# A two-layer hybrid decoder: GLA state products in halves, attention strips zeroed once, later holds for two mixer products

## Chip, core, metric

One core of one Trainium2 chip runs the whole program. The metric is the device time of one execution in microseconds; the median of the runs counts.

## What is computed

Two layers of a decoder on 512 tokens of width 2048, in float32. Each layer normalises its input, multiplies it with one wide matrix, feeds slices of the result to four mixers (Conformer convolution, RG-LRU, sparse attention, gated linear attention), gates and joins their outputs and multiplies them with a second matrix.

```python
h = rmsnorm(x, pre_g)
proj = h @ w_in                      # 2048 -> 5916, split among the mixers and their gates
o_a = gla_mixer(...); o_b = rglru_mixer(...); o_c = nsa_mixer(...); o_d = conformer_mixer(...)
mixed = group_rmsnorm(concat(o_a, o_b, o_c, o_d), branch_g) * silu(z)
x = x + rmsnorm(mixed @ w_out, post_g)
```

The change is in the GLA mixer, which works in 8 chunks of 64 tokens, with 4 heads of 64 key and 128 value channels:

```python
attn = where(causal, q_dec @ (k * exp(-bcum)).T, 0)        # within a chunk
dstate = (k * exp(b_last - bcum)).T @ v                    # what a chunk adds to the state
state = decay * state + dstate                             # chunk after chunk
o = attn @ v + q_dec @ state_before
```

## The kernel before

Every large product is made three times in a reduced float32 format: an operand is split into a high half (a copy on ScalarE, ACT) and a low half (a difference on VectorE, DVE, or GpSimd, POOL), and `mm3` (L227) adds high x high, high x low and low x high. In the profile H and L are the halves of the layer's input, whi and wlo those of the weights, shi and slo those of mixer data. GLA's own products run in full float32; one shows as two records of PE.

A layer goes like this: four columns of the Conformer's gate (tiles f), then columns of 128 outputs one after another (`proj`, L277, tile pfm), each of 16 blocks of the 2048 inputs, 3 products a block. Column numbers count these from 0: 0 to 3 Conformer values, 4 to 7 RG-LRU, 8 to 11 attention keys and values, 12 and 13 queries, 14 to 17 GLA queries and keys, 18 and 19 queries, 20 to 35 the gates z. A block of token-major columns (tm) and the GLA values (gv) stand in between. The output projection (out_ps) ends the layer; its first two columns are taken up to the 12th block before the last four blocks, which are GLA's.

The mixers are generators; `advance` (L267) lets the first in the list run a few steps between columns. Who stands where in an engine's queue is then decided by the scheduler of the tile framework from priorities and its own model of durations: weight loads and their splits have the band "first", the weight products the band "last", mixer work lies between. PE's weight products therefore fill what mixers leave.

`LAG` (L62) names four places where mixer products are held by hand: with `late` (L215) they are put down, and `release` (L220) makes them follow one given product of a column, (column, block). Held are the Conformer's variance sum, the first of its pointwise products (pw_ps), the first transposes of GLA (klt_ps0) and the first state product (ds_ps).

`gla` (L600) works on two pairs of heads, p = 0 and 1. For each: decays (ga, gb, gm, ge), decayed queries gqz and keys gkd, then transposed keys (klt_ps, copied to gklt), scores of two heads (at_ps, L668), each head's scores written through a causal mask into a strip gat that GpSimd has zeroed (L664, L665, L670), seven state products (ds_ps, L681) whose results DVE adds to the running state gsp (L686, L134), and outputs (go_ps) from gat and from gqz with gsp. State products contract 64 rows: even chunks lie on rows 0 to 63 of PE, odd ones on rows 64 to 127. The strips come from a ring of five buffers, tag "pt", which weights, sums and attention use too; "qg" is a ring of four that holds the halves of the second query pair.

After `gla` its output is normalised (`group_norm`, L296: square, sum on PE gn_ps, square root on ACT, reciprocal on DVE), gated on POOL, and split by `put_h` (L255) into the halves that the output projection reads.

Of the kernel before, what the change touches and what calls it, by code (L numbers as in the profile page):

```python
# [21 lines left out]
P = 128  # L22
# [26 lines left out]
CONF, LRU, NSA, GLA = range(4)  # L49
# [9 lines left out]
PS_A, PS_B = (0, 1, 2, 3, 4, 5), (0, 3)  # L59


LAG = {"var_ps": (13, 13), "pw_ps": (15, 1), "klt_ps0": (31, 15), "ds_ps": (32, 4)}  # L62


class Trunk:
# [148 lines left out]
    @contextmanager  # L214
    def late(self, name):  # L215
        self.lag = name if name in LAG else None
        yield
        self.lag = None

    def release(self, ins, col, k):  # L220
        for name, at in LAG.items():
            if at == (col, k):
                for i in self.held.pop(name, ()):
                    self.tc.add_manual_dep(i, ins.name, mybir.DependencyInfo(
                        mybir.DependencyClass.NoSync, mybir.DependencyReason.DATA), reason="late")
# [374 lines left out]
    def gla(self, qk, gv, fg):  # L600
        dve, act, gp = self.dve, self.act, self.gp
        wfg = self.strip("pt", "wfg", 512)
        self.nc.sync.dma_start(wfg[:96, :256], self.a["w_fg2"][self.l])
        wf3 = self.strip("pt", "wf3", 512, F32R)
        self.high_low_high(wf3[:96, :256], wfg[:96, :256], dve)
        fg3 = self.strip("pt", "fg3", 512, F32R)
        self.high_high_low(fg3[:, :384].rearrange("p (b r n) -> p b r n", b=4, r=3),
                           fg.rearrange("p (b n) -> p b n", b=4), 16, dve)
        spt = self.quad("x0", "gsp")
        qzt = self.quad("x1", "gqz")  # L610
        Y = self.Y[GLA] = self.quad("t3", "ygla")
        pf = self.bank("fg_ps")
        for b in range(4):
            self.tr(pf[:96, b * P:(b + 1) * P], fg3[:, b * 96:(b + 1) * 96].bitcast(F32), self.ident)
        fgT = self.strip("pt", "fgT", 512, F32R)
        act(fgT[:96], pf[:96, :], AF.Copy)
        pfg = []
        for p in range(2):
            ps = self.bank("fg2_ps")
            self.mm(ps, wf3[:96, p * P:(p + 1) * P], fgT[:96])  # L620
            pfg.append(ps)
        for p in range(2):
            q, k = [qk[:, (2 * p + i) * 512:(2 * p + i + 1) * 512] for i in range(2)]
            ps = pfg[p]
            bf = self.col(V_BFG + p)
            a_, m_, b_, e_ = [self.strip("yv", n) for n in ("ga", "gm", "gb", "ge")]
            act(a_, ps, AF.Abs, bias=bf)
            self.ts(dve, m_, ps, bf, 0.0, ALU.add, ALU.min)
            act(a_, a_, AF.Exp, scale=-1.0)
            act(a_, a_, AF.Ln, bias=self.one)  # L630
            gp.tensor_sub(m_, m_, a_)
            gp.memset(e_, 1.0)
            gp.memset(e_.rearrange("p (c t) -> p c t", c=8)[:, :, 0:1], 0.0)
            dve.tensor_tensor_scan(b_, e_, m_, 0.0, op0=ALU.mult, op1=ALU.add)
            yield 3.0
            b3 = b_.rearrange("p (c t) -> p c t", c=8)
            act(a_, b_, AF.Exp, scale=1.0 / 16)
            a3 = a_.rearrange("p (c t) -> p c t", c=8)
            dec = self.sm.tile([P, 8], F32, tag="dec", name="dec")
            dve.tensor_copy(dec, a3[:, :, 63])  # L640
            qz = qzt[:, 1024 * p:1024 * p + 1024]
            qd = qz.rearrange("p (c h t) -> p c h t", c=8, h=2)
            gp.memset(qz, 0.0)
            for h in range(2):
                r = slice(64 * h, 64 * h + 64)
                dve.tensor_mul(qd[r, :, h, :], q[r].rearrange("p (c t) -> p c t", c=8), a3[r])
            yield 2.0
            act(e_, b_, AF.Exp, scale=-1.0 / 16)
            kd = self.strip("pt", "gkd")
            gp.tensor_mul(kd, k, e_)  # L650
            dve.tensor_sub(m_.rearrange("p (c t) -> p c t", c=8), b3[:, :, 63:64].to_broadcast([P, 8, 64]), b3)
            act(m_, m_, AF.Exp, scale=1.0 / 16)
            gp.tensor_mul(k, k, m_)
            ps = self.bank("klt_ps")
            with self.late(f"klt_ps{p}"):
                for b in range(4):
                    self.tr(ps[:, b * P:(b + 1) * P], k[:, b * P:(b + 1) * P], self.ident)
            klT = self.strip("pt", "gklt")
            act(klT, ps, AF.Copy)
            yield 3.0  # L660
            at = []
            for h in range(2):
                r = slice(64 * h, 64 * h + 64)
                t = self.strip("pt", f"gat{h}")  # L664
                gp.memset(t, 0.0)  # L665
                ps = self.bank("at_ps")
                for b in range(4):
                    self.mm(ps[:, b * P:(b + 1) * P], kd[r, b * P:(b + 1) * P], qd[r, 2 * b:2 * b + 2, h, :],  # L668
                            b == 0, b == 3, skip_group_check=True)
                dve.copy_predicated(t.rearrange("p (b c) -> p b c", b=4),  # L670
                                    self.glam[:, None, :].to_broadcast([P, 4, P]),
                                    ps.rearrange("p (b c) -> p b c", b=4))
                at.append(t)
                yield 2.0
            sp = spt[:, 1024 * p:1024 * p + 1024].rearrange("p (c e) -> p c e", c=8)
            for c in range(7):
                ps = self.bank("ds_ps")
                r = slice(64 * (c % 2), 64 * (c % 2) + 64)
                b = c // 2
                with self.late(None if p + c else "ds_ps"):  # L680
                    self.mm(ps[:, :256], klT[r, b * P:(b + 1) * P], gv[r, 512 * b + 256 * p:512 * b + 256 * p + 256])  # L681
                for h in range(2):
                    r = slice(64 * h, 64 * h + 64)
                    d = ps[r, h * P:(h + 1) * P]
                    if c == 0:
                        dve.tensor_copy(sp[r, c + 1], d)  # L686
                    else:
                        self.stt(sp[r, c + 1], sp[r, c], dec[r, c:c + 1], d, ALU.mult, ALU.add)
                yield 1.5
            for i in range(2):  # L690
                po = self.bank("go_ps", self.op, "op")
                o4 = po.rearrange("p (h c t) -> p h c t", h=2, c=4)
                for h in range(2):
                    for b in range(2):
                        v0 = 512 * (2 * i + b) + (2 * p + h) * P
                        self.mm(po[:, h * 256 + b * P:h * 256 + (b + 1) * P], gv[:, v0:v0 + P],
                                at[h][:, (2 * i + b) * P:(2 * i + b + 1) * P], h + b == 0, False,
                                skip_group_check=True)
                for c in range(4):
                    if i + c > 0:  # L700
                        self.mm(o4[:, :, c, :], sp[:, 4 * i + c], qd[:, 4 * i + c], False, c == 3,
                                skip_group_check=True)
                for h in range(2):
                    c0 = (2 * p + h) * 512 + 256 * i
                    act(Y[:, c0:c0 + 256], po[:, h * 256:(h + 1) * 256], AF.Copy)
                yield 3.0
        yield from self.group_norm(GLA)
# [44 lines left out]
    def layer(self, l, xs):  # L752
        nc, a, dve, act, gp = self.nc, self.a, self.dve, self.act, self.gp
# [11 lines left out]
        first = [self.bank(f"f{i}", self.acc, "acc") for i in range(4)]  # L765
# [8 lines left out]
        for u, t in steps:  # L774
# [7 lines left out]
            for k in (2 * u, 2 * u + 1):  # L782
# [3 lines left out]
                with self.band("last"):  # L786
                    for i in range(4):
# [3 lines left out]
                                 skip_group_check=len(halves) > 1)  # L791
# [21 lines left out]
        for c in range(4):  # L813
            yv = self.strip("yv", "yv", 542)
            gp.memset(yv[:, :30], 0.0)
            ps = self.bank("pfm") if c < 2 else None
# [53 lines left out]
        for i, c in enumerate((NSA_KC, NSA_VC, NSA_KS, NSA_KW)):  # L870
            self.scaled(kv[i], self.proj(c))
            if i >= 2:
                hv, lv, zv = [t.rearrange("p (j r) -> p j r", j=4) for t in (KH, KL, kv[i])]
                r = slice((i - 2) * P, (i - 1) * P)
# [24 lines left out]
        for p in range(2):  # L899
            for i, (c, s) in enumerate(((GLA_Q, 0.125), (GLA_K, 1.0))):  # L900
                ps = self.proj(c + p * P)
# [3 lines left out]
        gv = self.quad("t6", "gv")  # L905
# [43 lines left out]
            self.load_vec(l + 1)  # L949
        M, N = [None] * KT, [None] * KT  # L950
        for i in range(KT):
            self.put_h(M, N, i, self.Y[i // 4][:, (i % 4) * 512:(i % 4 + 1) * 512], None)


        xs = [self.quad(tag, "xs") for tag in self.XTAGS]
# [153 lines left out]
```

## Time and profile before

| | |
|---|---|
| runs | 1632.26 to 1633.25 us, median 1632.89 |
| profiled execution | 1629.83 us |
| its span, first to last instruction | 1628.0 us |
| PE, DVE, ACT, POOL busy | 98%, 63%, 45%, 29% of the span |
| mean granted clock of PE | 0.994 |
| data moved | 165.54 MB, mean 102 GB/s |

Busy is not bound: PE's matmuls overlap, so that the distance of their starts is their price, and the ends that the profile shows are modelled. Idle time of the other engines costs nothing as long as PE does not wait for them.

### The profile page before, as it was taken

To read this page: it belongs to the slowest core of one execution; us is meant where nothing else is said; L and a number is where in the kernel's file an instruction comes from. 1 tells how busy PE (TensorE), PEld (TensorE's weight loads), DVE (VectorE), ACT (ScalarE), POOL (GpSimd) and SP (SyncE) were. 2 spreads that over 40 slices of the span, in tenths; PEclk is the share of its full clock that TensorE was granted. 3 is DMA by queue.
4 is the path that set the end of the run, shared out by engine and by line. 5 is a ranking of instruction groups with operands and counts; after the bars stand their busy time and mean duration, and the time that the engine had idled before them with its cause. 6 is when DMAs were issued, how large, how long until landed. Compare 5 with 4: busy or idle time off the path is not lost.

```text
span 1628.0 us, 22310 instructions
## 1 busy us (share of the span) xinstructions
PE 1591.1 (98%) x8380; PEld 1351.7 (83%) x8380; DVE 1024.5 (63%) x1654; ACT 727.1 (45%) x1313; POOL 471.9 (29%) x399
## 2 busy tenths in 40 slices
PE   8999999999999999999989999999999999999996
PEld 6889887998888777888888898879988887788886
DVE  8588986478564758111496889854976667571114
ACT  7322465454455635333453224654544555453331
POOL 1452242212123413222145522411121235132223
PEclk9999999999999999999999999999999999999998
DMA  7322322422112213442333222234221212134323
GB/s 251 104 92 83 117 78 99 158 75 88 53 66 69 90 53 128 157 136 98 111 130 110 99 90 91 91 117 143 78 74 57 78 59 77 63 117 155 121 99 117
DMA packets 54861, 165.54 MB, mean 102 GB/s; under 512 B 5920, under 2 KB 14816, under 8 KB 54752
## 3 DMA queue, kind: packets, MB, share of 16 engines
q1 hardware_dynamic: 53376, 162.79, 29.9%
q8 instruction: 66, 1.08, 0.3%
q10 hardware_dynamic: 1376, 1.31, 0.2%
q14 instruction: 43, 0.35, 0.1%
HBM read 155.69 MB, written 8.39 MB: 101 GB/s over the span
## 4 chain that ended last, share of the span: by engine, by line
PE 88%; DVE 7%; ACT 2%; DMA 2%; issue 1%; POOL 0%; SPq 0%; DVEq 0%; POOLq 0%; ACTq 0%
PE pfm L203 44%; PE out_ps L203 20%; PE gv L203 6%; PE tm L203 3%; PE f L203 2%; PE o_ps L203 2%; PE s_ps L203 2%; PE pw_ps L203 1%; DVE L L134 1%; PE go_ps L203 1%; PE pt_ps L209 1%; DVE wlo L148 1%; PE ch_ps L203 1%; PE ds_ps L203 1%; PE gn_ps L203 1%
## 5 line engine op out<-in xcount | busy, mean ns | idle before, releaser
L147 ACT ACTIVATE whi<-raw 128x512 fp32r<-128x512 f32 (+1 forms) x506 | 309.3, 616 | 615.5 <-PE pfm L203 305.6
L148 POOL TENSOR_TENSOR wlo<-raw,whi 128x512 fp32r<-128x512 f32 (+1 forms) x211 | 276.5, 1311 | 805.1 <-ACT whi L147 761.9
L203 PE MATMUL pfm<-H,whi 128*128 128x512 f32 x1152 | 452.7, 393 | 0.0
L203 PE MATMUL pfm<-H,wlo 128*128 128x512 f32 x1152 | 452.0, 392 | 0.3 <-POOL wlo L148 0.3
L203 PE MATMUL pfm<-L,whi 128*128 128x512 f32 x1152 | 452.0, 392 | 0.0
L148 DVE TENSOR_TENSOR wlo<-raw,whi 128x512 fp32r<-128x512 f32 (+1 forms) x295 | 225.8, 769 | 318.9 <-ACT whi L147 308.5
L203 PEld LDWEIGHTS pfm<-H,wlo 128*128 128x128 f32 x1152 | 216.7, 188 | 46.3 <-issue 1.0
L203 PEld LDWEIGHTS pfm<-H,whi 128*128 128x128 f32 x1152 | 216.6, 188 | 44.9 <-issue 0.7
L203 PEld LDWEIGHTS pfm<-L,whi 128*128 128x128 f32 x1152 | 216.6, 188 | 44.7 <-issue 0.4
L203 PE MATMUL out_ps<-L,whi 128*128 128x512 f32 (+1 forms) x552 | 200.9, 364 | 0.7 <-DVE L L262 0.7
L203 PE MATMUL out_ps<-H,wlo 128*128 128x512 f32 (+1 forms) x552 | 200.7, 365 | 0.0
L203 PE MATMUL out_ps<-H,whi 128*128 128x512 f32 (+1 forms) x552 | 200.3, 365 | 0.0
L134 DVE SCALAR_TENSOR_TENSOR cv_ps<-yv,vec,cv_ps 128x512 f32<-128x512 f32 x232 | 175.0, 754 | 6.8
L203 PEld LDWEIGHTS out_ps<-L,whi 128*128 128x128 f32 x552 | 104.0, 188 | 17.7 <-DVE L L262 1.1
L203 PEld LDWEIGHTS out_ps<-H,whi 128*128 128x128 f32 x552 | 104.0, 188 | 16.7
L203 PEld LDWEIGHTS out_ps<-H,wlo 128*128 128x128 f32 x552 | 104.0, 188 | 16.4
L234 DVE RECIPROCAL gn_ps<-gn_ps 128x512 f32<-128x512 f32 x32 | 107.4, 3356 | 9.6 <-ACT gn_ps L233 9.6
L203 PE MATMUL gv<-wlo,H 128*128 128x256 f32 x256 | 72.7, 284 | 0.0
L203 PE MATMUL gv<-whi,L 128*128 128x256 f32 x256 | 72.6, 284 | 0.0
L203 PE MATMUL gv<-whi,H 128*128 128x256 f32 x256 | 72.3, 284 | 0.0
L203 PE MATMUL f<-H,whi 128*128 128x256 f32 (+1 forms) x192 | 56.0, 326 | 7.4 <-ACT whi L147 7.4
L203 PE MATMUL f<-L,whi 128*128 128x256 f32 (+1 forms) x192 | 59.4, 326 | 2.3 <-DVE L L134 2.3
(293 smaller groups left out, 2313.9 us busy)
## 6 DMA issues: line engine op xcount, KB each, us to landing
raw<-w_in SPq DMA_DIRECT2D x175, 512.0 KB, 3.2
raw<-w_out SPq DMA_DIRECT2D x64, 512.0 KB, 3.7
mraw<-cmp_w SPq DMA_DIRECT2D x16, 512.0 KB, 3.6
raw<-w_tm SPq DMA_DIRECT2D x16, 284.0 KB, 2.8
xs<-xT SPq DMA_DIRECT2D x16, 256.0 KB, 6.0
xs<-xT SPq DMA_DIRECT2D x8, 512.0 KB, 4.7
x_scratch<-xs SPq DMA_DIRECT2D x16, 256.0 KB, 2.2
xs<-x_scratch SPq DMA_DIRECT2D x8, 512.0 KB, 4.7
```

The costliest lines, as they stand in the source:

```text
L134: self.dve.scalar_tensor_tensor(out, in0, s, in1, op0=op0, op1=op1)
L147: self.act(hi, src, AF.Copy)
L148: eng.tensor_sub(lo, src, hi.bitcast(F32))
L203: ins = self.nc.tensor.matmul(out, lhsT, rhs, start=start, stop=stop, **kw)
L209: ins = self.nc.tensor.transpose(out, src, ident)
L234: self.dve.reciprocal(out, out)
```

## The change

Four edits. Two of the holds in `LAG` move: the pointwise products from block 1 to block 5 of column 15, the first state product from block 4 to block 7 of column 32. Each state product of 64 x 256 becomes two of 64 x 128, into the same bank. The four masked strips of a layer are taken from "qg" and zeroed at the start of `gla`, in place of two from "pt" zeroed for each pair. The splits of the four GLA strips for the output projection get the band "first".

```diff
-LAG = {"var_ps": (13, 13), "pw_ps": (15, 1), "klt_ps0": (31, 15), "ds_ps": (32, 4)}
+LAG = {"var_ps": (13, 13), "pw_ps": (15, 5), "klt_ps0": (31, 15), "ds_ps": (32, 7)}
...
+        gat = [self.strip("qg", "gat") for _ in range(4)]
+        for t in gat:
+            gp.memset(t, 0.0)
...
-                t = self.strip("pt", f"gat{h}")
-                gp.memset(t, 0.0)
+                t = gat[2 * p + h]
...
-                    self.mm(ps[:, :256], klT[r, b * P:(b + 1) * P], gv[r, 512 * b + 256 * p:512 * b + 256 * p + 256])
+                    for h in range(2):
+                        v0 = 512 * b + (2 * p + h) * P
+                        self.mm(ps[:, h * P:(h + 1) * P], klT[r, b * P:(b + 1) * P], gv[r, v0:v0 + P], h == 0, h == 1,
+                                skip_group_check=True)
...
-            self.put_h(M, N, i, self.Y[i // 4][:, (i % 4) * 512:(i % 4 + 1) * 512], None)
+            with self.band("first") if i // 4 == GLA else nullcontext():
+                self.put_h(M, N, i, self.Y[i // 4][:, (i % 4) * 512:(i % 4 + 1) * 512], None)
```

Since the scheduler works the order out anew, more moves than the edits say. PE in layer 0 at the pointwise products, before (H0 and H1 are blocks 0 and 1 of the input):

```order
L203 MATMUL pfm_2546<-H0_118,wlo_2550 128x512
L203 MATMUL pfm_2546<-H1_134,whi_2549 128x512
L203 MATMUL pfm_2546<-L1_135,whi_2549 128x512
L203 MATMUL pfm_2546<-H1_134,wlo_2550 128x512
L203 MATMUL pw_ps_1924<-shi_1937,mhi_1930 128x512
```

and now:

```order
L203 MATMUL pfm_2546<-H4_206,wlo_2554 128x512
L203 MATMUL pfm_2546<-H5_222,whi_2553 128x512
L203 MATMUL pfm_2546<-L5_223,whi_2553 128x512
L203 MATMUL pfm_2546<-H5_222,wlo_2554 128x512
L203 MATMUL pw_ps_1924<-shi_1937,mhi_1930 128x512
```

Blocks 2 to 5 of the same column, 12 products, now stand ahead of the first pointwise product.

PE in layer 1 behind the first GLA scores (at_ps), before; 15 weight products stand between the scores and the first ds_ps:

```order
L203 MATMUL ds_ps<-gv,gklt 128x256
L203 MATMUL pfm<-H_6927,whi 128x512
L203 MATMUL pfm<-L_6928,whi 128x512
L203 MATMUL ds_ps<-gv,gklt 128x256
L203 MATMUL go_ps<-gat_12170,gv 128x128
L203 MATMUL ds_ps<-gv,gklt 128x256
L203 MATMUL go_ps<-gat_12170,gv 128x128
L203 MATMUL go_ps<-gat_12178,gv 128x128 x2
```

and now; 19 weight products stand between the scores and the go_ps:

```order
L203 MATMUL pfm<-H_6948,whi 128x512
L203 MATMUL go_ps<-gat,gv 128x128 x4
L203 MATMUL pfm<-L_6949,whi 128x512
L203 MATMUL pfm<-H_6948,wlo 128x512
L203 MATMUL pfm<-H_6952,whi 128x512
L203 MATMUL pfm<-L_6953,whi 128x512
L203 MATMUL pfm<-H_6952,wlo 128x512
L203 MATMUL ds_ps<-gv,gklt 128x128 x6
```

The four output products that read the masked strips now come first and together; behind them the halves of three state products stand in one group. Further on a second group of six halves and one of two end the pair.

ACT in layer 0 at the end of GLA, before (ygla<-go_ps are copies of GLA's outputs, the last pair here; gn_ps is the square root of the normalisation's first strip):

```order
L147 ACTIVATE whi<-raw 128x512
L147 ACTIVATE shi<-sq 128x512
L705 ACTIVATE ygla<-go_ps 128x256 x2
L233 ACT_TABLE_LOAD
L233 ACTIVATE gn_ps<-gn_ps,eps 128x512
```

and now:

```order
L710 ACTIVATE ygla<-go_ps 128x256 x2
L147 ACTIVATE whi<-raw 128x512
L233 ACT_TABLE_LOAD
L233 ACTIVATE gn_ps<-gn_ps,eps 128x512
L710 ACTIVATE ygla<-go_ps 128x256 x2
```

The square root of the first strip, with its table, now stands ahead of the copies of the last outputs; layer 1 has the same two orders.

## Rows read from the trace of the kernel before

**Rows 1.** The page's first part: PE, busy us, share of the span, instructions.
```profile
PE 1591.1 (98%) x8380; PEld 1351.7 (83%) x8380; DVE 1024.5 (63%) x1654; ACT 727.1 (45%) x1313; POOL 471.9 (29%) x399
```
**Rows 2.** Waits of PE: whom it waited for, us in total, times, longest.
```profile
PE pw_ps L203 <- ACT shi L147: 2.3, 2, 1.6
...
PE ds_ps L203 <- DVE gat L670: 2.1, 1, 2.1
```
**Rows 3.** The chain that ended last, layer 0: start us, us, what.
```profile
56.37 87.04 PE pfm L203 x384
```
**Rows 4.** Timeline of PE, layer 0: start, us, instruction, [idle before, releaser].
```profile
252.95 0.39 PE L203 MATMUL pfm<-H,wlo 128*128 128x512 f32 x1
254.95 0.50 PE L203 MATMUL pw_ps<-shi,mhi 128*128 128x512 f32 x1 [1.61 <-ACT shi L147]
255.81 0.50 PE L203 MATMUL pw_ps<-slo,mhi 128*128 128x512 f32 x1 [0.36 <-DVE slo L148]
```
**Rows 5.** Stretches: length, busy us of PE, PEld, DVE, ACT, POOL, clock, DMA.
```profile
257.03:260.43 3.40, 3.40 (x9) 2.63 (x9) 1.86 (x4) 1.96 (x3) 0.66 (x1) 0.50 0.46 154
1376.60:1380.00 3.40, 3.40 (x12) 2.48 (x12) 1.14 (x4) 0.00 (x0) 3.40 (x4) 0.50 0.00 0
```
**Rows 6.** Timelines of ACT and DVE, layer 0: halves of the second pointwise input.
```profile
258.33 0.63 ACT L147 ACTIVATE shi<-sy 128x512 fp32r<-128x512 f32 x1
259.00 0.69 DVE L148 TENSOR_TENSOR slo<-sy,shi 128x512 fp32r<-128x512 f32 x1 [1.54 <-ACT shi L147]
```
**Rows 7.** Timeline of PE, layer 1, the same pointwise products.
```profile
1060.68 0.39 PE L203 MATMUL pfm<-H,wlo 128*128 128x512 f32 x1
1061.76 0.49 PE L203 MATMUL pw_ps<-shi,mhi 128*128 128x512 f32 x1 [0.69 <-ACT shi L147]
1063.14 0.50 PE L203 MATMUL pw_ps<-slo,mhi 128*128 128x512 f32 x1 [0.89 <-DVE slo L148]
...
1066.44 0.50 PE L203 MATMUL pw_ps<-slo,mhi 128*128 128x512 f32 x1 [0.23 <-DVE slo L148]
```
**Rows 8.** Timeline of PE, layer 0, GLA: scores, a lone state product, two side by side.
```profile
559.74 1.71 PE L203 MATMUL at_ps<-gqz,gkd 64*128 64x128 f32 x16
561.38 0.50 PE L203 MATMUL pfm<-H,whi 128*128 128x512 f32 x1
...
564.70 0.39 PE L203 MATMUL pfm<-H,wlo 128*128 128x512 f32 x1
565.02 0.70 PE L203 MATMUL ds_ps<-gv,gklt 64*128 64x256 f32 x2
...
565.98 0.40 PE L203 MATMUL pfm<-L,whi 128*128 128x512 f32 x1
...
588.26 0.70 PE L203 MATMUL ds_ps<-gv,gklt 64*128 64x256 f32 x4
```
**Rows 9.** Timeline of PE, layer 1, first state products.
```profile
1370.94 0.39 PE L203 MATMUL pfm<-H,wlo 128*128 128x512 f32 x1
1371.83 0.69 PE L203 MATMUL ds_ps<-gv,gklt 64*128 64x256 f32 x2 [0.50 <-ACT gklt L659]
...
1372.79 0.40 PE L203 MATMUL pfm<-L,whi 128*128 128x512 f32 x1
1375.29 0.70 PE L203 MATMUL ds_ps<-gv,gklt 64*128 64x256 f32 x2 [2.10 <-DVE gat L670]
```
**Rows 10.** Timeline of DVE: the masked copies of the first pair, layers 0 and 1.
```profile
564.48 1.35 DVE L670 COPY_PREDICATED gat<-consts,at_ps 128x512 f32<-128x512 uint32 x2
...
1374.51 1.33 DVE L670 COPY_PREDICATED gat<-consts,at_ps 128x512 f32<-128x512 uint32 x2
```
**Rows 11.** Timeline of PE, layer 0, output projection at GLA's first block.
```profile
644.01 0.39 PE L203 MATMUL out_ps<-L,whi 128*128 128x512 f32 x1
645.12 0.51 PE L203 MATMUL out_ps<-L,whi 128*128 128x512 f32 x1 [0.72 <-DVE L L262]
```
**Rows 12.** Groups by shape, POOL: busy us, mean ns, idle before and releasers.
```profile
L665 POOL MEMSET gat<- 128x512 f32 x8 | 4.1, 524 | 14.0 <-PE ds_ps L203 10.1 <-PE go_ps L203 3.9
```

## The prediction

> **What bounds the kernel now.** The page's first part comes first: TensorE (PE) is busy 1591.1 us, 98% of the span [rows 1]. The other engines have room, so a change is worth what it takes from PE's own stream or from the few microseconds in which PE stands. The chain that ended last shows the stream: 384 weight products in 87.04 us, 0.2267 us each [rows 3]; this is my unit for "so many products later". The list of PE's waits is read next. At the start of a layer PE waits for weights, which nothing here touches. In the middle the longest are for mixer work: the Conformer's pointwise products (pw_ps) for their input, 2.3 us, and the GLA state products (ds_ps) for the masked copy of the scores, 2.1 us [rows 2]. PE's timeline tells which layer they are in, and the table of stretches shows what they cost beyond themselves: the granted clock is 0.50 (1.2 of 2.4 GHz) for 3.40 us behind the wait in layer 0's pw_ps, and again for 3.40 us behind the one in layer 1's ds_ps [rows 5]. PE is busy through both slow stretches, so each costs half of it, 1.7 us.
>
> All sums are made against the profiled execution's own 1629.83 us. The median of the three runs is 3.06 us above it, and I add that at the end. 0.2%, 3.3 us, is about what a measurement of this kernel can tell from no change.
>
> **Pointwise products, layer 0.** From 252.95 to 254.95 us is one product and 1.77 us of standing, from 254.95 to 255.81 one product (0.23) and 0.63 [rows 4]; with 1.7 for the clock the place costs 4.1. The hold moves from block 1 to block 5 of column 15, 4 blocks of 3 products, 12 x 0.2267 = 2.72 us. PE would have been free at 252.95 + 0.23 = 253.18, so it now comes to these products at 255.90. Both halves of the first input are there by 255.81. The second input is needed 12 products later, at 0.235 each: 258.72. Its high half was done at 258.33 + 0.63 = 258.96, its low half at 259.00 + 0.69 = 259.69 [rows 6]. Neither hangs on the hold, and both engines have the same order up to there. So PE still stands 0.24, then 0.5: 0.7 us, less than layer 1's stretch bears today without a slow clock. Saved: 3.4.
>
> **Pointwise products, layer 1.** From the idle times and starts, PE stands 0.85, 1.15 and 0.40 us [rows 7], together 2.4, with no slow clock. Coming 2.72 us later it finds the first two gone, and the second low half, which let PE go at 1066.44, is asked for at about 1066.7. Saved: 2.4. What was queued behind: the compression and everything after it start 12 products later, counted in weight products, and their own weights with them. Up to the end of GLA this is worked back to between 5 and 8 products.
>
> **State products, the stream.** Today each stands almost alone among the weight products. One such place costs, from 564.70 to 565.98, 1.28 less two weight products, 0.83 us [rows 8]. Of that, streaming is 0.41: the sixteen score records of 128 columns take 561.38 - 559.74 = 1.64 us, 0.1025 each, and two products of 128 are four such records [rows 8]. The other 0.42 is paid for going into 64-row products and out of them. So two of 128 cost what one of 256 did. What changes is the order: it now has the first pair's seven as three, three and one. Two state products on different halves of the rows run side by side: a group of four records shows 0.70 us, as a group of two does [rows 8]. A group of three is then 0.42 + 2 x 0.41 = 1.24, and the seven are 1.24 + 1.24 + 0.83 = 3.3 instead of 7 x 0.83 = 5.8: saved 2.5 in each layer. If the split halves do not run side by side, a group is 0.42 + 3 x 0.41 = 1.65 and 1.7 is saved; I take 2.5, since the score products of both row halves overlap too, and keep 1.7 for the range. In layer 0 the second pair's scores are cut once more by an output product, as layer 1's are already: 0.4 lost, 2.1 saved there.
>
> The Trainium skill speaks against the split: by the page TensorEngine Tiling (Array Packing), section Performance Considerations, each matmul carries an overhead of some 60 cycles. As an estimate from that page, 56 more records at 25 ns would be 1.4 us, and the sum would end at 1623.7. The 0.1025 us per record of [rows 8] does not agree: such records leave no room for it.
>
> **State products, layer 1, the wait.** PE stands 0.6 us ahead of 1371.83 and 2.2 ahead of 1375.29 [rows 9]; with the clock's 1.7, 4.5. The hold is 9 products later, but the wait is not for the zeroing, which is what the new strips remove: VectorE comes to the masked copies only at 1374.51 and ends at 1375.84 [rows 10], with its own work ahead of them, and its order ahead of them is the same in the change. Now look at what PE asks first: four output products (go_ps) on the masked scores stand 4 products behind the place of the first state product of before, and they are not held. PE was through at 1370.94 + 0.23 = 1371.17, so it asks at 1372.1. The first copy is done at about 1375.2: PE stands 3.1 us, and 0.2 for the second copy. I also keep the slow clock, 1.7, because this is the longest single wait of the four places. 5.0 in place of 4.5: 0.5 lost. In layer 0 the copies end at 564.48 + 1.35 = 565.83 [rows 10]; PE, which left the scores at 561.38 [rows 8], asks 19 products later, at 565.8: nothing.
>
> **Zeroing, on GpSimd.** The number of zeroings stays at four a layer; they move ahead, behind the last score product of attention, with weight splits queued behind them. They take 4 x 0.524 = 2.1 us [rows 12]. PE needs the next of those splits 65 products (14.7 us) behind that score product, so this is hidden; were the cover gone, it would cost at most 2.1 a layer.
>
> **GLA copies.** PE stands 1.11 - 0.23 = 0.9 us in layer 0 for the low half of the first GLA strip [rows 11]. The priority itself moves a single copy on ScalarE and none on VectorE. But the square root of the normalisation now stands ahead of the last output copy, so that VectorE's long reciprocals begin sooner, measured by PE, by those eight output products at least: 16 x 0.1025 = 1.6 us. Saved: 0.9; bounds 0 and 0.9, apart from the rival below.
>
> **Sum.** 3.4 + 2.4 + 2.1 + 2.5 - 0.5 + 0.9 = 10.8. 1629.83 - 10.8 = 1619.0, and with 3.06 **1622 us**.
>
> **Rivals.**
> 1. *The wait in layer 1 goes too.* If the masked copies come over 3 us sooner, PE never stands there. VectorE has a chain to go through before the masked copies, and part of its input comes from GpSimd. For it: two zeroings are gone from GpSimd's queue right there. Against: the pieces and their order on VectorE are the same, and its next piece waits for nothing up to 1374.51 [rows 10]. It gives 5.0 more: 1617. Chance 0.20.
> 2. *The end of GLA is late.* Its last outputs come 5 (layer 0) and 8 (layer 1) products later, 1.1 and 1.8 us, and if the normalisation does not begin sooner, the output projection waits for it: 0.9 kept, 1.1 and 1.8 added, and a slow clock behind both, 3.4. That is 7.2 worse: 1629.5. For it: PE is at the edge there already [rows 11]. Against: the order on ScalarE. Chance 0.12.
> 3. *The holds do nothing*: the pointwise inputs move back with the products. The forecast's 5.8 is lost: 1628. Against: nothing that feeds them is held. Chance 0.08.
> 4. *Slower: each half pays its own way in and out of the 64-row mode.* Place: the 56 halves. Price: 28 more times 0.42, and the 4.6 saved by grouping is gone, 11.8 + 4.6 = 16.4 worse: 1638.5. It turns the sign from about 0.25 us for each added product, if grouping gains nothing. Against: the score records, 16 in a row at 0.1025 [rows 8], pay once. Chance 0.05. The Trainium skill, same page, section Key Properties, has it that a change of the tiling mode drains TensorE and a change of the tile alone does not; by that rule this rival cannot happen, and the trace agrees with it, with 0.70 us for four records on two row halves as for two on one.
>
> **How the numbers follow.** The forecast has 0.55. Faster by over 0.2% (under 1629.6): the forecast, rivals 1 and 3, and half of rival 2, whose time is right at the bound: 0.89. Within 0.2%: the other half, 0.06. Slower: rival 4, 0.05. The forecast's own bounds are 1620 (no slow clock in layer 1) to 1624.5 (halves not side by side, copies not sooner). The range takes in rivals 1 and 3 and half of 2: 1616 to 1629.
>
> **What would show it.** In the profile after: no slow clock near the pointwise products of layer 0, and waits there under 1 us in all; no wait in layer 1's; the state products in groups of 6, 6 and 2 with about 1.25 us for a group of six; a wait of PE at go_ps for the masked copy of about 3 us in layer 1, with or without a slow clock behind it; no wait of out_ps for L. I am wrong if that go_ps wait is missing, if out_ps waits over 1 us, or if a lone pair of halves costs over 1 us.

## The result, and the profile after

The changed kernel takes 1622.21 us (median of six runs, 1621.61 to 1624.16). The kernel before, run beside it, takes 1632.49. The ratio is 0.9939, 95% interval 0.9930 to 0.9949: 10.3 us faster. The profiled execution took 1622.29 us, its span is 1620.1 us. PE is still busy nearly all the time [rows 1]:

```profile
PE 1585.7 (98%) x8436; PEld 1355.2 (84%) x8436; DVE 1027.0 (63%) x1654; ACT 726.2 (45%) x1313; POOL 476.3 (29%) x399
```

PE's list of waits in the changed kernel (whom it waited for, us in total, times, longest) answers to [rows 2]. Of the pointwise products' waits 0.4 us are left, out_ps has none, and the state products' wait is now one of go_ps:

```profile
PE go_ps L203 <- DVE gat L672: 4.2, 1, 4.2
...
PE pw_ps L203 <- DVE slo L148: 0.2, 1, 0.2
PE pw_ps L203 <- ACT shi L147: 0.2, 1, 0.2
```

PE's timeline of the changed kernel in layer 0, pointwise products [rows 4]: the first input is there when PE comes; the second is late in two short steps, in front of the products at 259.96 and 260.69.

```profile
256.58 0.39 PE L203 MATMUL pfm<-H,wlo 128*128 128x512 f32 x1
256.81 0.40 PE L203 MATMUL pw_ps<-shi,mhi 128*128 128x512 f32 x1
...
259.37 0.40 PE L203 MATMUL pw_ps<-shi,mlo 128*128 128x512 f32 x1
259.96 0.49 PE L203 MATMUL pw_ps<-shi,mhi 128*128 128x512 f32 x1 [0.19 <-ACT shi L147]
260.69 0.50 PE L203 MATMUL pw_ps<-slo,mhi 128*128 128x512 f32 x1 [0.23 <-DVE slo L148]
```

The same timeline further on, layer 0's GLA: a group of six halves (twelve records) among weight products. From 565.58 to 567.32 there are 1.74 us, less two weight products 1.29.

```profile
565.58 0.39 PE L203 MATMUL pfm<-H,wlo 128*128 128x512 f32 x1
565.89 1.16 PE L203 MATMUL ds_ps<-gv,gklt 64*128 64x128 f32 x12
566.98 0.50 PE L203 MATMUL pfm<-H,whi 128*128 128x512 f32 x1
567.32 0.40 PE L203 MATMUL pfm<-L,whi 128*128 128x512 f32 x1
```

And layer 1's GLA, where [rows 9] stood. From 1363.96 to the masked outputs go_ps PE spends 4.58 us in place of one product's 0.23:

```profile
1363.96 0.39 PE L203 MATMUL pfm<-H,whi 128*128 128x512 f32 x1
1368.54 2.07 PE L203 MATMUL go_ps<-gat,gv 128*128 128x128 f32 x8 [4.19 <-DVE gat L672]
1370.26 0.77 PE L203 MATMUL pfm<-L,whi 128*128 128x512 f32 x1
```

Two stretches of the changed kernel (length, busy us of PE, PEld, DVE, ACT, POOL, granted clock, DMA) answer to [rows 5]. At the pointwise products of layer 0 the clock is full. In layer 1 it is 0.50 for 6.82 us, of which PE works 4.64, so that it loses 2.3:

```profile
257.00:260.40 3.40, 3.21 (x13) 2.06 (x11) 1.85 (x2) 1.93 (x3) 0.85 (x1) 1.00 0.41 143
1366.36:1373.18 6.82, 4.64 (x17) 3.71 (x19) 2.73 (x5) 3.06 (x3) 3.92 (x4) 0.50 0.21 77
```

### The profile page after: what moved, and what is told of

The parts are those of the page before. It is cut to its first block, busy times and chain, and to the rows that moved or that the text cites. A ratio compares the mean times of both kernels' runs of the same rounds, so it can differ in the third digit from the quotient of the medians.

```text
span 1620.1 us, 22403 instructions
## 1 busy us (share of the span) xinstructions
PE 1585.7 (98%) x8436; PEld 1355.2 (84%) x8436; DVE 1027.0 (63%) x1654; ACT 726.2 (45%) x1313; POOL 476.3 (29%) x399
## 4 chain that ended last, share of the span: by engine, by line
PE 91%; DVE 5%; ACT 1%; DMA 1%; issue 1%; POOL 1%; SPq 0%; DVEq 0%; POOLq 0%; ACTq 0%
PE pfm L203 46%; PE out_ps L203 22%; PE gv L203 6%; PE tm L203 3%; PE f L203 3%; PE o_ps L203 2%; PE s_ps L203 2%; PE pw_ps L203 1%; PE go_ps L203 1%; PE pt_ps L209 1%; DVE L L134 1%; PE ch_ps L203 1%; PE gn_ps L203 1%; PE ds_ps L203 1%; DVE wlo L148 1%
```

## The experiments

One part of the change stands in no experiment: without the band "first" for the GLA strips every engine's instructions stand in exactly the same order, so it moves nothing here.

### A second profile of the kernel before

No edit. The first profile of before lay 2.7 us under the median of its runs, and the question was where.

> The kernel before once more, unchanged, for a second profile of it. Theory: layer 1's wait for the masked copy hangs on a chain that begins with the landing of a weight transfer at ScalarE (2.17 us of waiting in the profile before, 4.5 in the changed kernel and in three others); the profile before was an execution in which it landed 1.2 us sooner, and with the shorter slow clock that followed (3.4 against 6.8 us long) it lay 3 us below its own median. Then this profile shows a wait of about 1.7 us for gklt, 2.1 for gat, a slow clock of 6.8 us and a time near 1632.5. Rival (the profile before was typical, and the time that PE gained upstream is what makes the transfer late): gklt 0.5, slow clock 3.4 us, as before.

Measured: 1632.47 us, profiled and median. PE's waits in this second profile of before, with the one for gklt that had been 0.50 in [rows 9]:

```profile
PE ds_ps L203 <- DVE gat L670: 2.1, 1, 2.1
...
PE ds_ps L203 <- ACT gklt L659: 1.8, 1, 1.8
```

Its stretch of slow clock behind them, in place of the 3.40 us of [rows 5]:

```profile
1376.35:1383.17 6.82, 6.40 (x17) 4.49 (x18) 2.82 (x8) 1.60 (x2) 5.67 (x5) 0.50 0.15 57
```

From the 100th weight product on, the two executions keep within 0.1 us of one shift up to there (0.25 us at the last scores) and are 2.82 apart ten weight products on; nothing further on brings that back. So 2.6 us of the 2.66 between the first profile and the median were one place. ScalarE's timelines show its head: the weight copy ahead of GLA's first decay (ga) waits for its transfer, first in the profile before, then in the second, then in the changed kernel:

```profile
1349.97 0.63 ACT L147 ACTIVATE whi<-raw 128x512 fp32r<-128x512 f32 x1 [2.17 <-DMA raw<-w_in]
```
```profile
1351.46 0.64 ACT L147 ACTIVATE whi<-raw 128x512 fp32r<-128x512 f32 x1 [4.59 <-DMA raw<-w_in]
```
```profile
1343.22 0.63 ACT L147 ACTIVATE whi<-raw 128x512 fp32r<-128x512 f32 x1 [4.57 <-DMA raw<-w_in]
```

Behind it comes GLA's own chain (ga, gm, gb, gqz, the masked copies), so 1.2 us at its head are 1.2 us at PE. The rival, that the time gained upstream makes the transfer late, falls: the kernel before has it too.

### The later pointwise hold alone

```diff
-LAG = {"var_ps": (13, 13), "pw_ps": (15, 1), "klt_ps0": (31, 15), "ds_ps": (32, 4)}
+LAG = {"var_ps": (13, 13), "pw_ps": (15, 5), "klt_ps0": (31, 15), "ds_ps": (32, 4)}
```

> The kernel before with one edit: the pointwise products held to block 5 of column 15 in place of block 1. Theory (each edit pays in its own place): the two stretches of pointwise products get 3.1 and 2.6 us cheaper, as in the changed kernel, and the normalisation behind GLA now comes ahead of its last outputs here too, so the 0.9 us wait of out_ps goes: 6.6 us faster, about 1625.9 (ratio 0.996). The slow clock behind layer 0's pointwise products is gone, the one behind layer 1's state products stays. Rival (the pointwise inputs move back with the products, and the gain comes from GLA): 0 to 1 us, 1632. Rival (the changed kernel's whole gain is the holds, GLA gives nothing): 10 us, 1622.

Measured: 1627.89 (1626.45 to 1629.31), ratio 0.9973, 0.9963 to 0.9984: 4.4 us faster. The expectation counted on the normalisation standing ahead of GLA's last outputs. That order comes with the new strips and is not this kernel's: out_ps still waits 0.7 us, so 5.7 was to be expected. From the 100th weight product on, its profile gains 6.2 us on the second profile of before; it lost 1.5 ahead of that, at the start of the program, where nothing differs and the clock is at 0.50 for 3.41 us. PE's waits for the pointwise inputs are down to one of 0.2. Both rivals fall: the inputs don't move back, and the hold isn't the whole gain.

### The split alone

```diff
-                    self.mm(ps[:, :256], klT[r, b * P:(b + 1) * P], gv[r, 512 * b + 256 * p:512 * b + 256 * p + 256])
+                    for h in range(2):
+                        v0 = 512 * b + (2 * p + h) * P
+                        self.mm(ps[:, h * P:(h + 1) * P], klT[r, b * P:(b + 1) * P], gv[r, v0:v0 + P], h == 0, h == 1,
+                                skip_group_check=True)
```

> The kernel before with one edit: each state product as two of 128 columns. Theory: the scheduler now puts six halves in a group at the hold (before: one product), so that fewer groups go into 64-row mode; grouping saves 1 to 2.5 us a layer. In layer 1 the masked outputs (go_ps) stand 15 weight products and the first group behind the scores, 1 us earlier than in the changed kernel, so PE waits 5 us there with 3.4 us lost to a slow clock behind it, where before lost 4.5 in all: 3.9 worse. The pointwise waits stay. Sum: between 2 faster and 2 slower, 1631 to 1635. Rival (each half pays 0.42 us for its own way into the mode): 12 to 16 slower, 1645 or more. Rival (the split gives the changed kernel's gain): 7 or more faster, 1625.

Measured: 1633.44, ratio 1.0007, 0.9998 to 1.0016: no difference that can be measured, as the theory had it. 28 more products that each paid 0.42 would have cost 12 us. In layer 1 it is the state products that wait, 1.7 us for gklt and 2.7 for gat, and not the masked outputs, as had been expected.

### The change without the split

The same lines the other way round, on the changed kernel.

> The changed kernel with each state product in one of 256 columns again, holds, strips and bands as in the change. In order the first pair has groups of 3, 2, 1 and 1 products where the changed kernel has halves in 6, 6 and 2; the second pair is cut as often in both. Theory (a group costs 0.42 us and 0.41 for each pair of halves, whatever their size): one group more a layer, 0.4 to 0.9 us slower in each, and the same wait of go_ps and slow clock in layer 1: 1623 to 1624, ratio to the changed kernel 1.0005 to 1.001. Rival (the split is what gains): 4 us or more slower. Rival (the split costs its overheads and the holds gain): 1 to 2 us faster than the changed kernel, 1620.5.

Measured: 1623.47, ratio to before 0.9948, 0.9936 to 0.9961. That is 1.3 us above the changed kernel, with overlapping intervals, so that the times alone do not show a difference. In the profiles it is 1.0 (from 0.37 behind to 1.38 at the end) from layer 1's GLA on and 1.2 (0.72 ahead to 0.46 behind) over layer 0's with the edge behind it. That is the theory's size, but one group less is not shown to be the reason. In layer 0 GLA itself loses 0.1 and the output projection 1.1: out_ps waits 0.4 us for L again. In layer 1 the first pair has the same three groups as with halves; the loss comes behind the second pair's scores, where the state products stand in six groups in place of four. The price of a group does show here. Three whole products at the same place, from 565.05 to 566.75, cost 1.70 - 0.45 = 1.25, the six halves above 1.29:

```profile
565.05 0.39 PE L203 MATMUL pfm<-H,wlo 128*128 128x512 f32 x1
565.36 1.13 PE L203 MATMUL ds_ps<-gv,gklt 64*128 64x256 f32 x6
566.42 0.50 PE L203 MATMUL pfm<-H,whi 128*128 128x512 f32 x1
566.75 0.40 PE L203 MATMUL pfm<-L,whi 128*128 128x512 f32 x1
```

Six more records cost 0.04. The Trainium skill, page TensorEngine Tiling (Array Packing), section Performance Considerations, gives each matmul an overhead of some 60 cycles; as an estimate from that page, taking the overhead as added to each product, the six would have cost 0.15. The trace does not agree with that reading.

### The change with the early hold of the state products

```diff
-LAG = {"var_ps": (13, 13), "pw_ps": (15, 5), "klt_ps0": (31, 15), "ds_ps": (32, 7)}
+LAG = {"var_ps": (13, 13), "pw_ps": (15, 5), "klt_ps0": (31, 15), "ds_ps": (32, 4)}
```

> The changed kernel with the hold of the first state product back at block 4 of column 32. In order the halves still come in sixes, and the four masked outputs stand behind the first six, some 5 us behind the scores in place of 4.3. Theory: what PE waits for in layer 1 is the masked copy, whose time this hold does not set; the wait is 4 to 5 us again with the same slow clock, layer 0 gets a wait of up to 1 us: 0 to 1.5 us slower than the changed kernel, 1622 to 1624. Rival (the later hold is what makes the groups, or what made PE wait in layer 1): without it layer 1 is 3 to 7 us faster or slower.

Measured: 1625.91, ratio 0.9965, 0.9953 to 0.9978: 3.7 us slower than the changed kernel, where the theory had 1.5 at most. PE's timeline in layer 1:

```profile
1367.22 0.71 PE L203 MATMUL ds_ps<-gv,gklt 64*128 64x128 f32 x4 [1.80 <-ACT gklt L662]
1370.66 1.83 PE L203 MATMUL ds_ps<-gv,gklt 64*128 64x128 f32 x8 [2.74 <-DVE gat L672]
1372.42 2.07 PE L203 MATMUL go_ps<-gat,gv 128*128 128x128 f32 x8
```

The waits sum to 4.5, the slow clock is 6.83 us long again; that part was right. Up to the end of the second pair's scores layer 1's GLA loses 1.4 us. What was missed is the second pair itself: behind its scores its state products now stand in five places among the weight products in place of two, and cost some 2.5 us more. So the rival has a part in it: the later hold does make groups. The profiled execution is 2.3 us above the median of its runs, and 1.3 us of its loss stand at the start of layer 1, where nothing differs. The timeline shows something else: state products wait for the masked copy although they read none. The scores, the transposes and the state products take their PSUM banks from one ring of three (the pool mx); the first state product gets the bank of the transposes (free when gklt is copied), the second and third those of the scores (free when the masked copies have read them), by the kernel's text. That is also what the ds_ps of [rows 9] waited for.

### The change without strips of their own

```diff
-        gat = [self.strip("qg", "gat") for _ in range(4)]
-        for t in gat:
-            gp.memset(t, 0.0)
...
-                t = gat[2 * p + h]
+                t = self.strip("pt", f"gat{h}")
+                gp.memset(t, 0.0)
```

> The changed kernel with two masked strips zeroed anew for each pair, as before, from the ring they shared. In order PE and the masked copies stay where they are, but the normalisation stands behind GLA's last outputs again. Theory: zeroing itself is hidden, the go_ps wait in layer 1 stays 4.2; what the strips bring is the order at the end of GLA: here the normalisation begins 5 products later than before in layer 0, so out_ps waits for L, 0.9 + 1.1 = 2.0 us in layer 0 and up to 2 in layer 1: 1.5 to 5 us slower than the changed kernel, 1624 to 1627. Rival (the order at the end does not matter, the wait of before was the copies' priority): 0 to 0.3 slower, 1622.3. Rival (the zeroings sit in front of GpSimd's part of the masked copies' chain): the go_ps wait in layer 1 grows by 1 to 2 us.

Measured: 1629.38 (1624.97 to 1630.62), ratio 0.9971, 0.9959 to 0.9983: 7.2 us slower than the changed kernel, where 5 at most had been expected; its runs lie between 2.8 and 8.4 us above. In PE's waits whl are halves of output weights that lie in the buffers of mixer weights:

```profile
PE go_ps L203 <- DVE gat L670: 4.5, 2, 4.3
...
PE out_ps L203 <- ACT whl L147: 1.0, 1, 1.0
PE out_ps L203 <- DVE whl L148: 0.7, 1, 0.7
PE out_ps L203 <- DVE L L262: 0.6, 1, 0.6
```

The wait for the masked copy stays, so the zeroing was hidden. Layer 0's output projection waits for L, 1.3 us with what follows it. Layer 1's does not wait for L but for halves of its own weights (whl), and falls into a slow clock:

```profile
1448.98:1452.39 3.41, 3.41 (x9) 2.63 (x10) 3.41 (x3) 1.93 (x4) 3.41 (x3) 0.50 0.00 0
```

Together 4.1 us there. So the two places make 5.4 of the 7.3 us by which this profile is behind; 1.4 more is a slow clock at the start of layer 1, where nothing differs. ScalarE's timeline says why layer 1 waits: the copy of those weights is queued behind the Silu of GLA's gate (L947 here), which waits for VectorE's last piece of the gate. In the changed kernel the same Silu (L949) waits 6.50 us:

```profile
1444.96 1.92 ACT L947 ACTIVATE z<-z 128x2048 f32<-128x2048 f32 x1 [10.14 <-DVE z L294]
1446.78 0.61 ACT L147 ACTIVATE whl<-raw 128x512 fp32r<-128x512 f32 x1
```
```profile
1437.17 1.92 ACT L949 ACTIVATE z<-z 128x2048 f32<-128x2048 f32 x1 [6.50 <-DVE z L294]
1439.00 0.61 ACT L147 ACTIVATE whl<-raw 128x512 fp32r<-128x512 f32 x1
```

The first rival (the order at the end does not matter) falls, and so does the second (the zeroing delays the masked copies).

### The strips alone

The same lines the other way round, on the kernel before.

> The kernel before with one edit: the four masked strips of their own, zeroed once at the start of GLA. In order the state products stand alone as before, and the normalisation begins ahead of GLA's last outputs. Theory (the strips matter at the end of GLA, and there only where its end comes later than before): the 0.7 us wait of out_ps in layer 0 goes and nothing else moves; the waits for the masked copy in layer 1 stay 1.8 and 2.1: 1631.6, ratio 0.9995. Rival (the strips are worth 7 us by themselves, as taking them out of the changed kernel cost 7): 1625. Rival (zeroing on GpSimd ahead of the copies delayed them): layer 1's waits shrink by 1 us or more, 1629.

Measured: 1633.46, ratio 1.0005, 0.9996 to 1.0014: no difference. Layer 0's wait for L goes, as expected, but the same 0.7 us turns up in layer 1. There the wait for gklt is 0.7 and not 1.8, which looks like the second rival; but the transfer at the head of the chain landed early, as in the first profile (ScalarE waits 1.96 us for it), and from there to the masked copies it takes the same 24.55 us as in both profiles of before. So the strips are worth 5 to 7 us in the change and nothing that can be measured without it: they keep GLA's end ahead of the output projection where the later holds would have made it late.

### Holding the masked outputs

On the changed kernel, the first four masked outputs get a hold of their own; here at block 12, in the second kernel at block 14 with the state products at 13.

```diff
-LAG = {"var_ps": (13, 13), "pw_ps": (15, 5), "klt_ps0": (31, 15), "ds_ps": (32, 7)}
+LAG = {"var_ps": (13, 13), "pw_ps": (15, 5), "klt_ps0": (31, 15), "ds_ps": (32, 7), "go_ps": (32, 12)}
...
+                with self.late(None if p + i else "go_ps"):
```

> The changed kernel with a fifth hold: the first four masked outputs of GLA (go_ps) follow block 12 of column 32, 39 weight products behind the scores in place of 19; the state products keep their hold at block 7. Theory: in layer 1 the masked copies are done 8.7 to 9.3 us behind the scores and PE now asks after some 10; the 4.2 us wait of go_ps and the 6.8 us of slow clock behind it (half of it lost) both go: 7.6 us faster than the changed kernel, about 1614.6, ratio 0.989. Rival (a slow clock comes with this dense stretch whether PE waits or not): 4.2 faster, 1618. Rival (the outputs come late and hold up the second pair or the normalisation, so that a wait appears there): 1618 to 1622.

> The changed kernel with the first four masked outputs held to block 14 and the first state product to block 13 of column 32, so that the order ahead of the second pair is as in the change but some 25 products later. Theory: the same 7.6 us as with the holds at 12 and 7, less up to 1 us for the end of GLA, which comes 8 to 11 products (2 us) later and reaches the output projection's edge: 1614.5 to 1616. Rival (late outputs hold up the normalisation): out_ps waits for L by 1 to 2 us with a slow clock behind it, 1617 to 1620.

Measured: 1621.32 (ratio 0.9930, 0.9918 to 0.9943) and 1621.49 (0.9927, 0.9914 to 0.9941), both within 1 us of the changed kernel, with overlapping intervals, where 7.6 had been expected. With the first, the wait only moves to the state products, by way of the PSUM ring, and there is no slow clock there:

```profile
1364.29 0.71 PE L203 MATMUL ds_ps<-gv,gklt 64*128 64x128 f32 x4
1367.38 0.71 PE L203 MATMUL ds_ps<-gv,gklt 64*128 64x128 f32 x4 [2.39 <-DVE gat L672]
```

It gains 2.5 us over layer 1's GLA, and 1.2 of these go again where out_ps waits for L. With the second, go_ps waits no more, but the next state products wait 0.8 us for VectorE's sums and a slow clock of 3.41 us follows; 2.2 gained there. The expectation had taken all 6.8 us of slow clock as worked through, when PE stood for a third of it, and had not seen the ring.

### Moving the whole of GLA's first pair

On the changed kernel, transposes, scores and all that follows them come later, the first pair in the same order. The second edit gives the output projection more products ahead of GLA's blocks.

```diff
-LAG = {"var_ps": (13, 13), "pw_ps": (15, 5), "klt_ps0": (31, 15), "ds_ps": (32, 7)}
+LAG = {"var_ps": (13, 13), "pw_ps": (15, 5), "klt_ps0": (32, 6), "ds_ps": (32, 14)}
```
```diff
-        for m in range(2):
-            head.append((self.bank("out_ps", self.acc, "acc"), weights(m, ("mraw", "mhi", "mlo")[:3 * m])))
+        for m in range(3):
+            spare = ((), ("mraw", "mhi", "mlo"), (None, None, None, "yv"))[m]
+            head.append((self.bank("out_ps", self.acc, "acc"), weights(m, spare)))
...
-            if m < 2:
+            if m < 3:
+                if m == 2:
+                    load_rows(0)
```

> The changed kernel with GLA's first transposes held to block 6 of column 32 in place of block 15 of column 31, and the state products to block 14 in place of 7: the same order, 21 weight products (4.8 us) later. Theory: the masked copies come when VectorE's chain lets them, not when PE makes the scores; so the 4.2 us wait of go_ps in layer 1 shrinks to under 0.5 and its slow clock goes, 6.6 us gained (4.3 and half of the 4.6 us of slow clock that PE works through); at the end of GLA, which comes 14 to 17 products later, out_ps waits for L: 3 us in layer 0 and 2 to 4 in layer 1, possibly with a slow clock. Sum: 1620 to 1624. Rival (the copies move back with the scores): the wait of go_ps stays at 4, 1625 to 1630.

> The changed kernel with one edit behind GLA: the output projection takes three columns, in place of two, up to their 12th block before the last four blocks, which are GLA's. Theory: nothing waits at that edge in the changed kernel, so the 36 products (8.2 us) of slack that it adds are worth nothing by themselves: within 1 us of the changed kernel, 1621 to 1623. Rival (three heads make the weights of the fourth column late, through the rings of the weight halves): a wait of out_ps for whi or wlo, 1 to 4 us slower.

> Both: the later transposes and the three columns ahead of GLA's blocks. Theory: the 6.6 us of layer 1's go_ps wait and slow clock are gained, and the later end of GLA is covered by the 36 products more: 1615.6, ratio to the kernel before 0.990. Rival (the time that PE gains before the end of GLA is given back there in any case, since VectorE's normalisation sets it): out_ps waits for L by 2 us or more, 1619 to 1622.

Measured: the later pair alone 1615.89 (1615.17 to 1616.58, ratio 0.9897, 0.9884 to 0.9911), the three columns alone 1623.47 (0.9941, 0.9927 to 0.9954), both 1617.22 (0.9905, 0.9891 to 0.9918). The first is 6.3 us faster than the changed kernel, with intervals that don't touch: it beats both kernels, and lies under the 1620 to 1624 that were expected. PE and VectorE in layer 1 of it:

```profile
1368.18 0.40 PE L203 MATMUL pfm<-H,whi 128*128 128x512 f32 x1
1368.42 1.05 PE L203 MATMUL go_ps<-gat,gv 128*128 128x128 f32 x8
1369.23 0.48 PE L203 MATMUL pfm<-L,whi 128*128 128x512 f32 x1
```
```profile
1365.34 1.37 DVE L672 COPY_PREDICATED gat<-consts,at_ps 128x512 f32<-128x512 uint32 x2
```

The copies end 1.7 us before PE asks, and the clock stays full. In the profiles 4.9 us come from layer 1's GLA and 1.1 from layer 0's. The copies do not move back with the scores, and the theory that they come when VectorE's chain lets them holds. They even come 1.9 us sooner than in the changed kernel, counted from the same weight product. In the changed kernel GpSimd makes two products for the second pair (gkd and the keys of its state products, 1363.12 to 1366.09) while VectorE makes gqz and a low half of weights; here GpSimd does nothing from 1360.2 to 1367.3. The two lines of gqz, changed kernel and this one:

```profile
1362.58 2.39 DVE L649 TENSOR_TENSOR gqz<-qk,ga 64x512 f32<-64x512 f32 x2
```
```profile
1362.06 1.38 DVE L649 TENSOR_TENSOR gqz<-qk,ga 64x512 f32<-64x512 f32 x2
```

The low half behind it takes 1.64 and 0.69 us. So the 1.7 us to spare come of a shorter chain, which nobody had expected; the hold alone, 4.8 us later, would about have covered the 4.4 that PE stood. And out_ps does not wait at all, though GLA's last outputs come 23 (layer 0) and 13 (layer 1) weight products later: that edge had at least 2.9 us to spare in layer 1, and the three columns buy nothing. Why it waits in the kernels with held outputs and without the split, and not here, was not settled.

## Why the prediction was right

The forecast was 1622.0 (range 1616 to 1629); measured 1622.21. Since the second profile of before took what its runs take, the terms are read against that one: how far the changed kernel's PE is ahead at the same weight product, counted from the program's start. The sum is that of the unrounded values.

| stretch (weight products) | forecast | measured |
|---|---|---|
| start, untouched (0 to 100) | 0 | 0.6 lost |
| pointwise products, layer 0 (to 2300) | 3.4 | 3.3 |
| GLA, layer 0 (to 2495) | 2.1 | 1.5 |
| output projection, layer 0 (to 2700) | 0.9 | 1.2 |
| pointwise products, layer 1 (to 5850) | 2.4 | 2.7 |
| GLA, layer 1 (to 6110) | 2.0 | 2.5 |
| rest | 0 | 0.3 lost |
| sum | 10.8 | 10.4 |

**Pointwise products.** Right, with the residue: 0.24 and 0.5 us were forecast, 0.36 and 0.50 measured, as the distances from 259.37 to 259.96 and from there to 260.69 less one product of 0.23. There is no slow clock. Layer 0 gained 4.1 at first and gave 0.8 back among the attention's products, which the forecast did not have.

**State products.** A group of six was to cost 1.24 and cost 1.29. What the forecast put down to the order with the split can be had from either of two edits: layer 0's GLA gains 1.4 us without the split, as whole products form groups at the later hold as well, 1.25 with the split alone, and 1.5 with both. Undoing the hold costs 3.7 us; undoing the split costs 1.3, which is not clear of the scatter of the runs.

**The wait in layer 1.** This is where a step failed. The forecast had PE stand 3.1 us at go_ps and lose 1.7 to the clock; it stood 4.2 and lost 2.3. The step was to take the copies' time from one execution: in twelve of the fourteen profiles the transfer at the head of the chain lands some 1.2 us later against PE. The same holds for the place that it replaces, put at 4.5, which costs 7.0 in the second profile (1.75 and 2.08 of waiting, half of 6.40). So the forecast called this exchange a loss of 0.5 and it is a gain of 0.5.

**The 3.06 us added at the end.** That step was wrong as a mechanism and near in size: the first profile was not faster everywhere, but at this one place. The second profile of before and the changed kernel's both have the late transfer, so the difference of the medians is not the difference of the two first profiles, 7.5. Against that first profile, from whose rows the terms came, layer 1's GLA gains nothing (2.0 had been forecast) and the start loses 0.9; the 3.06, added for another reason, makes up for both. That the forecast lies within 0.2 us of the result is in part luck.

**The end of GLA.** The wait for L is gone, as forecast, but the margin was called 1.6 us and is at least 2.9. The rival priced at 7.2, in which the end of GLA is late, is what happens without the strips, by waits in both layers and a slow clock behind one; that it is 7.2 us there too is chance, since 1.4 of them stand elsewhere. The forecast gave the order on ScalarE as the reason against it, and that order hangs on the strips: without them ScalarE copies GLA's last outputs ahead of the first square root, as before. By the kernel's text, the strips leave the ring that the normalisation takes its buffers from, so that these come free ahead of GLA's last outputs. The single copy on ScalarE that the forecast gave to the priority is not there; the band moves nothing.

**The other rivals.** Layer 1's wait did not go, the holds did something, and no half pays its own way: 12 records of halves cost what 6 whole ones do.

**Slips in the sums.** Two of the times, 1623.7 and 1629.5, are 0.2 above what their terms give from 1622.1, and the place in [rows 9] comes to 4.6 and not 4.5. None of them changes the forecast.

## What to carry to other kernels

A wait found in one profile has a size of one execution: where it hangs on the landing of a transfer, take a second profile before pricing it, and look for the place when a profile is off its median. When a wait is moved by holding its reader, find what else holds the resource, here the PSUM bank of the scores; moving producer and reader together left the first pair's order intact and gained 6 us where holding the reader gained under 1. And an edit that measures nothing alone may be what lets another one keep its gain, so undo parts of a change as well as trying them alone.

## What the runs showed of the hardware that was not expected

The granted clock does not follow a wait by a fixed stretch: the same place in the kernel before had 3.40 us at 0.50 in one execution and 6.82 in another, where the waits ahead of it summed to 2.6 and 3.8 us; with the strips alone 2.8 us of waiting were followed by 6.83, and with the first held outputs 2.39 us by none. In the changed kernel it began while PE was still standing.

At the start of the program the 100th weight product comes between 33.5 and 35.6 us over the fourteen profiles. Four of them (the pointwise hold alone, the two kernels with three columns, the hold at block 14) are the latest, and in each the clock is at 0.50 for 3.4 us there, as in the three columns alone:

```profile
29.91:33.33 3.42, 3.42 (x10) 2.65 (x9) 3.42 (x6) 0.61 (x3) 1.36 (x3) 0.50 0.48 158
```

The start of layer 1 scatters in the same way: in five profiles (the split alone, the early hold, the kernel without strips, the later pair alone and with three columns) the clock is at 0.50 for 3.4 us somewhere between 804 and 855 us, in one of them twice, though no edit has its place there. A difference between two single profiles holds such pieces.

Elementwise work took longer where VectorE and GpSimd had it at once, as with gqz above. Ahead of the late transfer VectorE makes two low halves. In the profile before they come ahead of GpSimd's:

```profile
1345.42 1.27 DVE L148 TENSOR_TENSOR wlo<-raw,whi 128x512 fp32r<-128x512 f32 x2
```
```profile
1346.92 1.30 POOL L148 TENSOR_TENSOR wlo<-raw,whi 128x512 fp32r<-128x512 f32 x1 [9.56 <-ACT whi L147]
```

In the second profile one runs beside GpSimd's, and the two take 2.37:

```profile
1345.67 2.37 DVE L148 TENSOR_TENSOR wlo<-raw,whi 128x512 fp32r<-128x512 f32 x2
```
```profile
1346.00 1.49 POOL L148 TENSOR_TENSOR wlo<-raw,whi 128x512 fp32r<-128x512 f32 x1 [8.38 <-ACT whi L147]
```

That is 1.1 us more ahead of the issue of the transfer that GLA's chain waits for, which follows the low half at once. All fourteen profiles fall into these two cases: in the first one and with the strips alone the second low half takes 0.67 or 0.68 us and ScalarE waits 2.17 and 1.96 for the transfer; in the other twelve it takes 1.77 or 1.78 beside GpSimd's, and the wait is 4.4 to 4.7. That GpSimd's split is what makes VectorE's longer is argued, not shown: no run moved it alone.
